# Score products of the cross-attention by seven of eight in passes two to four, with folded weights made beside V

## The chip, the cores and the metric

The kernel runs on one core of a Trainium2 chip. A core has a matmul engine (TensorE, "PE" in the profile, with its weight loads as "PEld"), VectorE ("DVE"), ScalarE ("ACT"), GpSimd ("POOL") and SyncE ("SP"). Each engine takes its own instructions in order; they meet through semaphores. Most transfers are issued by SP, one after the other. The metric is the device time of one execution in microseconds. Three runs before the change took 2639.5, 2645.52 and 2638.56 us, median 2639.5.

## The reference

One layer of a hybrid encoder over 2048 tokens of 1024 channels:

```
y = rmsnorm(h) @ w_in                       # 1024 -> 2560: q, k, v (8 heads of 64), u (conv, 2 x 512)
att = dilated_sliding_attention(q, k, v)    # three patterns, softmax over each band
conv = conformer_conv(...)                  # gate, 31-tap depthwise conv, layernorm, silu
h = h + concat(att, conv) @ w_out
xq = rmsnorm(h) @ w_xq                      # 4 heads of 256
sc = (xq . xk) / sqrt(256); pr = softmax(sc); xo = pr @ xv    # 256 memory rows
h = h + xo @ w_xo
h = h + square(relu(rmsnorm(h) @ w_up)) @ w_down              # 1024 -> 4096 -> 1024
return rmsnorm(h)
```

All is float32 at the interface. The memory rows do not depend on the tokens, so the kernel folds `w_xq` with the keys into one matrix A (1024 x 4 heads x 256) and the values with `w_xo` into one matrix B. The score products that the change is about are h times A.

## The kernel before, in words

A float32 product is made as three float16 products: high by high, high by low, low by high (`mm3`, lines 374 to 376). Each operand is split beforehand into a float16 part (ACT) and the rest (DVE).

The program has a first phase over all tokens and then four passes of 512 tokens.

- **First phase.** The memory is folded into A (kept in DRAM as `ascr`, two pairs of heads) and B (`bscr`). The linears for k, q, the conv input (`glu`) and v (`lin_v`) run as a pipeline of units that PE takes in order. Beside it DVE runs the first conv tile (`cacc`), and `scan` loads `w_up`, `w_out` and `w_down` once to sum squares, from which `bounds` makes the power-of-two scales of all splits (`S_A` for A). V tiles `v0_0` to `v1_7` end this phase; each is read out by ACT and DVE into `vst` and stored to `vtok`.
- **Attention of the first pass** (`att(0)`, three patterns). It starts in the memory that the first phase's tiles leave; its masked score operation on DVE reads the tile `mask`, which SP loads. The remaining linears (`frest`: `u0_2`, `u0_3` and others, and `v1_8` to `v1_15`) are woven between its steps.
- **A pass** (`post(p)`). Stage o: `cat @ w_out` plus the residual, with `y`, the split input of the score products, as output. Stage xs: scores, 192 products of 512 columns a pass, A's tiles loaded from `ascr` and split anew in each pass (`ws_a`, by `wpost`). Softmax, transposes (`ptx`). Stage x: `probabilities @ B` plus the residual. Then the MLP, up and down. The attention and conv of the next pass are woven between these steps as side work; the fourth pass has none.
- **Seven of eight.** The MLP's up products of passes two to four already use a 2 x 2 block scheme with seven block products instead of eight (`quad`). Its weights' block sums are made once by `prep` on ACT and DVE and stored as `ust`; its input's block sums are made when the input is (`columns`, `put_columns`: `B11`, `B2`, `T1`, `T32`, `T4`).
- **Ring of weight tiles.** `wtile` gives out four or seven slots in turn (`ws`, and `raw` as the last three). In the first pass split weights of the MLP are also stored (`wst`) for later passes; `save(n)` issues the stores that are due, all but the last n.

The program's order is not the order on the engines: a scheduler places the instructions of each engine, within limits that `pinned`, `after` and `weave(main, (side, rate))` set.

Of the kernel before, what the change touches and what calls it, by code (L numbers as in the profile page):

```python
# [10 lines left out]
F32 = mybir.dt.float32  # L11
# [10 lines left out]
P = 128  # L22
# [26 lines left out]
def hybrid_layer(ctx, tc, A, out):  # L49
# [70 lines left out]
    ust = [[dr.tile([P, 2 * 1024], F16, name=f"ust{fg}_{i}") for i in range(7)] for fg in range(8)]  # L120
# [26 lines left out]
    gxm = cst.tile([P, 24], F32, name="gxm")  # L147
# [5 lines left out]
    cst.tile([P, 56], F32, name="cpad")  # L153
# [101 lines left out]
    def bounds():  # L255
# [9 lines left out]
        with ExitStack() as st:  # L265
# [15 lines left out]
            TS(c[18], c[18], 16.0, None, op0=ALU.mult)  # L281
# [11 lines left out]
        with ExitStack() as st:  # L293
# [14 lines left out]
            TS(gxm[:, 16:24], gxm[:, 8:16], -1.0, None, op0=ALU.mult)  # L308
        yield
# [153 lines left out]


# [544 lines left out]
    with ExitStack() as st:  # L1009
# [10 lines left out]
        weave(islice(steps, 5), (conv0, 1.05), (scn, 2))  # L1020
        frest = [u for c in range(4) for u in glu(c, (2, 3), True)]
        for u in frest[:2] * 2:
            next(u)
        weave(steps, (conv0, 1.05), (scn, 2))
        drain(conv0, scn)
# [347 lines left out]
    def flat(t):  # L1373
        return t.rearrange("p h a b -> p (h a b)")

# [133 lines left out]
    def resid_linear(load, rhs, korder, resid, hs, ssum, scale, gains, y, name, steps=False, wide=False, put=None):  # L1509
# [26 lines left out]
    def prep(fgs, q):  # L1536

        late = []

        def give(d, t):  # L1540
            late.append((d, t))

        def step():
            for d, t in late:
                dma(d, t, q)
            late.clear()

        def hi(o, i):
            ACT.activation(o, i, AF.Copy, scale=S_UP)

        def lo(o, i, h):
            DVE.scalar_tensor_tensor(o, i, S_UP, h, op0=ALU.mult, op1=ALU.subtract)

        for fg in fgs:
            for j in range(2):
                nm = f"{fg}{j}"
                raw = [ct0.tile([P, 8, P], F32, tag=f"ch{i}", name=f"pw{i}_{nm}") for i in range(2)]
                step()
                for i in range(2):
                    dma(raw[i], wcols(w_up, (4 * fg + 2 * i + j) * P), q)  # L1560
                a11, a12, a21, a22 = (r[:, 4 * i:4 * i + 4] for r in raw for i in range(2))
                yield
                yield
                step()
                t0 = ct0.tile([P, 2, 8, P], F16, tag="cl0", name=f"pt0_{nm}")
                hi(t0[:, 0], raw[0])
                s1 = sw.tile([P, 4, P], F32, tag="s1", name=f"ps1_{nm}")
                DVE.tensor_tensor(s1, a21, a22, op=ALU.add)
                DVE.tensor_tensor(a21, a11, a21, op=ALU.subtract)
                yield  # L1570
                step()
                lo(t0[:, 1], raw[0], t0[:, 0])
                give(ust[fg][j], flat(t0))
                DVE.tensor_tensor(a11, s1, a11, op=ALU.subtract)
                t2 = ct0.tile([P, 2, 8, P], F16, tag="cl1", name=f"pt2_{nm}")
                hi(t2[:, 0], raw[1])
                yield
                step()
                DVE.tensor_tensor(a12, a12, a11, op=ALU.subtract)
                lo(t2[:, 1], raw[1], t2[:, 0])  # L1580
                give(ust[fg][4 + j], flat(t2))
                yield
                step()
                t1 = ct0.tile([P, 2, 8, P], F16, tag="cl0", name=f"pt1_{nm}")
                hi(t1[:, 0, 0:4], a11)
                hi(t1[:, 0, 4:8], s1)
                t3 = sw.tile([P, 2, 4, P], F16, tag="s4", name=f"pt3_{nm}")
                hi(t3[:, 0], a12)
                yield
                step()  # L1590
# [588 lines left out]
```

## Time and profile before

| | |
|---|---|
| runs, us | 2639.5, 2645.52, 2638.56 |
| profiled execution | 2644.86 us, of which the span 2643.0 |
| granted clock, mean | 0.995 |
| busy PE, DVE, ACT, POOL | 98%, 74%, 47%, 12% of the span |
| chain that ended last | PE 77%, DVE 12%, DMA 6% |
| stage o of passes 1 to 4 begins at, us | 668.0, 1192.6, 1699.3, 2191.5 |
| stage xs | 713.6, 1234.9, 1746.7, 2236.8 |
| stage x | 767.9, 1290.9, 1796.1, 2281.2 |

The busy time of PE counts products that overlap: a product of 512 columns lasts 379 ns in the records, but the next begins earlier. The distance between two starts is the price of a product, and PE's idle time is seen best in the timeline. A row of a stage's table gives the length of the stretch, the busy time of each engine with its count of instructions, the granted clock, the DMA engines' mean busy share and the rate.

### The profile page before, as it was taken

How to read it: one execution, taken by the hardware profiler on the slowest of the kernel's cores; microseconds unless marked ns; L12 is line 12 of the kernel's file. 1: busy time of each engine (PE TensorE's matmuls, PEld its weight loads, DVE VectorE, ACT ScalarE, POOL GpSimd, SP SyncE). 2: the span in 40 equal slices, each digit the busy share in tenths (PEclk: the TensorE clock that was granted, in tenths of full speed). 3: DMA queues.
4: the chain of work that ended last, by engine and by line, in shares of the span. 5: the costliest groups of instructions: out<-in, count | busy, mean ns of one | idle time of the engine just before them, and what ended most of it. 6: DMA issues, size and time to landing. Idle time of an engine off the chain costs nothing.

```text
span 2643.0 us, 45573 instructions
## 1 busy us (share of the span) xinstructions
PE 2588.1 (98%) x17710; PEld 1650.8 (62%) x17710; DVE 1947.6 (74%) x3775; ACT 1239.1 (47%) x2194; POOL 307.3 (12%) x417
## 2 busy tenths in 40 slices
PE   8999999999999999999999999999999999999998
PEld 7844448777455555545576676555776664468886
DVE  5887756567667999775799986467899557675666
ACT  5737645376454345544553344255443234452323
POOL 1134101132100110110001111000110000000000
PEclk9999999999999999999999999999999999999999
DMA  8987977766634657785367677454686465345442
GB/s 263 300 266 221 284 233 258 194 177 189 186 98 139 193 175 244 219 271 162 108 213 218 200 240 238 165 162 132 216 264 192 145 203 167 100 133 170 156 138 78
DMA packets 401753, 509.51 MB, mean 193 GB/s; under 512 B 81181, under 2 KB 295121, under 8 KB 400768
## 3 DMA queue, kind: packets, MB, share of 16 engines
q1 hardware_dynamic: 380816, 446.35, 55.3%
q0 software_dynamic: 15536, 51.24, 6.0%
q10 hardware_dynamic: 5184, 9.01, 0.9%
q8 instruction: 139, 2.28, 0.4%
q14 instruction: 78, 0.64, 0.1%
HBM read 390.75 MB, written 115.75 MB: 192 GB/s over the span
## 4 chain that ended last, share of the span: by engine, by line
PE 77%; DVE 12%; DMA 6%; issue 2%; ACT 2%; SPq 0%; POOL 0%; DVEq 0%; POOLq 0%; ACTq 0%
PE dn L375 7%; PE dn L376 7%; PE dn L374 7%; PE up L376 6%; PE up L375 6%; PE up L374 6%; PE lin L376 3%; PE lin L374 3%; PE lin L375 3%; DVE cacc L391 3%; PE xs L375 2%; PE xs L376 2%; PE xs L374 2%; PE pt L1047 2%; PE o L374 2%
## 5 line engine op out<-in xcount | busy, mean ns | idle before, releaser
L391 DVE SCALAR_TENSOR_TENSOR cacc<-cu,cw,cacc 128x512 f32<-128x512 f32 x480 | 364.4, 765 | 5.5
L375 PE MATMUL dn<-hhl,ws_d 128*128 128x512 f16 x768 | 290.6, 379 | 1.4 <-DVE hhl L1878 0.8
L374 PE MATMUL dn<-hhh,ws_d 128*128 128x512 f16 x768 | 287.9, 379 | 3.7 <-ACT hhh L1655 2.3
L376 PE MATMUL dn<-hhh,ws_d 128*128 128x512 f16 x768 | 290.5, 379 | 0.0
L1040 DVE CUSTOM_DVE_ANT_0 sm<-s,mask,qks 128x256 f32<-128x256 f32 (+1 forms) x384 | 151.1, 433 | 31.6 <-PE s L1081 28.0
L1041 ACT ACTIVATE sm<-sm,o 128x256 f32<-128x256 f32 (+1 forms) x288 | 119.3, 455 | 110.9 <-DVE o L1040 110.3
L1051 DVE TENSOR_TENSOR pl<-pt,ph 128x512 f16<-128x512 f32 x160 | 109.7, 685 | 42.1 <-ACT ph L1050 41.7
L374 PEld LDWEIGHTS <-ws_t 128*128 128x128 f16 x1232 | 120.6, 98 | 18.2 <-DMA ws_t<-ust 1.8
L376 PEld LDWEIGHTS <-ws_d 128*128 128x128 f16 x768 | 75.1, 98 | 90.4 <-issue 2.0
L375 PEld LDWEIGHTS <-ws_t 128*128 128x128 f16 x1232 | 120.5, 98 | 17.5 <-issue 2.3
L1050 ACT CAST ph<-pt 128x512 f16<-128x512 f32 x160 | 91.4, 571 | 84.5 <-PE pt L1047 84.3
L376 PEld LDWEIGHTS <-ws_t 128*128 128x128 f16 x1232 | 120.5, 98 | 16.8 <-issue 1.1
L374 PEld LDWEIGHTS <-ws_d 128*128 128x128 f16 x768 | 75.1, 98 | 84.7 <-issue 2.5
L375 PEld LDWEIGHTS <-ws_d 128*128 128x128 f16 x768 | 75.4, 98 | 83.7 <-issue 1.6
L1904 DVE SCALAR_TENSOR_TENSOR h<-dn,bd,h 128x512 f32<-128x512 f32 x96 | 71.5, 746 | 74.0 <-PE dn L376 73.7
L1047 PE MATMUL pt<-ident,sm 128*128 128x128 f32 x640 | 98.2, 274 | 4.6 <-ACT sm L1041 2.9
L374 PE MATMUL up<-mh,ws_u 128*128 128x512 f16 x256 | 98.1, 383 | 2.1 <-DVE rl L1875 2.1
L1687 ACT ACTIVATE e<-e 128x512 f32<-128x512 f32 x88 | 55.2, 629 | 95.3 <-DVE e L1685 95.3
L376 PE MATMUL up<-mh,ws_u 128*128 128x512 f16 x256 | 98.1, 384 | 1.3 <-DVE ws_u L362 1.3
L375 PE MATMUL up<-ml,ws_u 128*128 128x512 f16 x256 | 98.1, 383 | 0.0
L374 PE MATMUL up<-T32h,ws_t 128*128 128x256 f16 x352 | 95.9, 273 | 2.1 <-DMA ws_t<-ust 2.1
L374 PE MATMUL o<-cath,ws_o 128*128 128x512 f16 x256 | 96.5, 379 | 0.9 <-ACT cath L1219 0.8
(560 smaller groups left out, 7751.3 us busy)
## 6 DMA issues: line engine op xcount, KB each, us to landing
ws_t<-ust SPq DMA_DIRECT2D x154, 512.0 KB
ws_d<-wst SPq DMA_DIRECT2D x80, 512.0 KB
ust<-pt POOLq DMA_DIRECT2D x36, 512.0 KB, 5.1
scan<-in_w_up_dram SPq DMA_DIRECT2D x32, 512.0 KB
scan<-in_w_down_dram SPq DMA_DIRECT2D x32, 512.0 KB
raw_o<-in_w_out_dram SPq DMA_DIRECT2D x32, 512.0 KB
raw_a<-ascr SPq DMA_DIRECT2D x32, 512.0 KB
raw_b<-bscr SPq DMA_DIRECT2D x32, 512.0 KB
```

The source lines that it names most:

```text
L374: PE.matmul(o, lh, rh, start=first, stop=False, skip_group_check=more)
L375: PE.matmul(o, lh, rl, start=False, stop=False, skip_group_check=more)
L376: last["pe"] = PE.matmul(o, ll, rh, start=False, stop=end, skip_group_check=more)
L391: DVE.scalar_tensor_tensor(acc, u[:, t:t + 512], cw[:, c, t:t + 1], acc, op0=ALU.mult, op1=ALU.add)
L1040: last["dve"] = DVE.tensor_tensor_reduce(dst, so, mask[:, 256 * m:256 * m + nk], SCORE, 3e38, ALU.add, ALU.min, mn)
L1041: last["act"] = ACT.activation(dst, dst, AF.Exp, bias=mn, scale=-1.0)
L1047: last["pe"] = PE.transpose(pt[:, j, :], sm[:, j, :], ident)
L1050: ACT.copy(ph, pt)
L1051: DVE.tensor_tensor(pl, pt, ph, op=ALU.subtract)
L1687: ACT.activation(e, e, AF.Square)
L1904: last["dve"] = DVE.scalar_tensor_tensor(hs[m], pt, K_DN, hs[m], op0=ALU.mult, op1=ALU.add)
```

## The change

1. In passes two to four the score products go by seven block products of eight (`side_quad`), with 256 columns each. The input is made as column blocks (`columns(p, "s")`, `put_columns` with the gain columns of the cross norm), the softmax and the transposes work on blocks (`soft_block`, `turn_block`). Pass one is as before.
2. The block sums of A are made once, by `prep((8, 9))` in the first phase, beside the V products; their tiles are those of the q weights (`q0` to `q3`) and temporaries. `side_scale` makes `S_A` ahead of `bounds`, and A's bound is four times as large to leave room for the sums. They are stored as `ust[8]` and `ust[9]`.
3. The first pass's last split MLP tile is stored at the end of that pass (`save(0)`) instead of at the second pass's first MLP tile.

```
-    ust = [[dr.tile([P, 2 * 1024], F16, name=f"ust{fg}_{i}") for i in range(7)] for fg in range(8)]
+    ust = [[dr.tile([P, 2 * 1024], F16, name=f"ust{fg}_{i}") for i in range(7)] for fg in range(10)]
...
-            TS(c[18], c[18], 16.0, None, op0=ALU.mult)
+            TS(c[3], c[3], 4.0, None, op0=ALU.mult)
+            for i in (17, 18):
+                TS(c[i], c[i], 16.0, None, op0=ALU.mult)
...
+    def side_scale():
+        c = bd[:, 59:60]
...
+            PE.matmul(pc[:, 0:n], onesq, acc2[:, AS[0]:AS[1]], start=True, stop=True)
+            DVE.tensor_reduce(c, pc[:, 0:n], axis=AX.X, op=ALU.add)
+            DVE.tensor_scalar(c, c, 4.0, None, op0=ALU.mult)
+        yield
+        pow2(S_A, I_A, None, 32768.0, "dve", of=c)
...
     (prep, moved up and given an allocator; its new lines)
+                    if fg < 8:
+                        dma(raw[i], wcols(w_up, (4 * fg + 2 * i + j) * P), q)
+                    else:
+                        v = ascr[fg - 8].rearrange("p (h j k) n -> p h j k n", h=2, j=2)
+                        dma(raw[i].rearrange("p (h k c) m -> p h k (c m)", h=2, k=2),
+                            v[:, :, j, :, 256 * i:256 * i + 256], q)
...
+        def side_tile(tag, shape, dtype, name):
+            at = {"ch0": "q0", "ch1": "q1", "cl0": "q2", "cl1": "q3"}.get(tag)
+            return wqk.tile(list(shape), dtype, tag=at, name=name) if at else t2(name, dtype, shape)
+
+        side = pinned(chain(side_scale(), prep((8, 9), None, side_tile)), "dve", "act")
...
-        weave(steps, (conv0, 1.05), (scn, 2))
-        drain(conv0, scn)
+        weave(steps, (conv0, 1.05), (scn, 2), (side, 3))
+        drain(conv0, scn, side)
...
-        y = ytiles("y")
+        y = put = None
+        if p:
+            one, two_, side = columns(p, "s")
+            put = put_columns(one, two_, hs, 0, 24)
+        else:
+            y = ytiles("y")
...
+        def side_quad(hp, pth, ptl):
...
+            def prod(pt, w, n, more=False):
+                for t in range(2):
+                    ts_ = slice(P * t, P * t + P)
+                    for k in range(4):
+                        wh, wl = (x.rearrange("p (k c) m -> p k (c m)", k=2)[:, k % 2] for x in w[k // 2])
+                        mm3(halved(pt)[:, t], side[n]("h", k)[:, ts_], side[n]("l", k)[:, ts_], wh, wl,
+                            not (more or k or t), k == 3, bool(more or t))
...
+            def done(e, pt, i, z):
+                last["dve"] = DVE.tensor_tensor(e, e, pt, op=ALU.add)
+                soft_block(e, z)
+                late.append((pth, ptl, i, z, e))
...
+            prod(X, w11, "B11")
+            e1 = kept(X, "e1")
+            prod(Y, w12, "B21")
...
+            if p:
+                for _ in side_quad(hp, pth, ptl):
+                    if mlp and hp:
+                        next(mlp)
+                    yield
+                continue
...
         r = rstd_from(fsum)
+        save(0)
```

Where the instructions stand. First DVE at the end of the V phase, before the change: `vst1_7` is the read-out of the last V tile of the phase, `u0_2` and `u0_3` are the gated linears' read-outs, and the ISA row is the attention's first masked score (numbers behind the names are buffer numbers).

```order
L817 SCALAR_TENSOR_TENSOR vst1_6_5257<-v1_6_5232,vst1_6_5257 128x4x64
L817 SCALAR_TENSOR_TENSOR vst1_7_5287<-v1_7_5262,vst1_7_5287 128x4x64
L746 SCALAR_TENSOR_TENSOR u0_2_5418<-sig0_2_5362,lin_5391 128x512
L746 SCALAR_TENSOR_TENSOR u0_3_5446<-sig0_3_5389,lin_5421 128x512
L817 SCALAR_TENSOR_TENSOR vst1_8_5476<-v1_8_5449,vst1_8_5476 128x4x64
L1040 ISA sm_5519,o3_00_5518<-s_5520,mask_5306,qks_269 128x128
```

The same place on DVE after the change: `ps1_91`, `pw0_91`, `pw1_91` and `pt.._91` are the sums, the loaded blocks and the split results of the fourth and last unit of block sums.

```order
L525 TENSOR_TENSOR pw1_91_5398<-pw0_91_5397,pw1_91_5398 128x512
L503 SCALAR_TENSOR_TENSOR pt2_91_5410<-pw1_91_5398,bd_277,pt2_91_5410 128x1024
L503 SCALAR_TENSOR_TENSOR pt0_91_5403<-pw0_91_5397,bd_277,pt0_91_5403 128x1024
L530 TENSOR_TENSOR pw0_91_5397<-ps1_91_5405,pw0_91_5397 128x512
L535 TENSOR_TENSOR pw0_91_5397<-pw0_91_5397 128x512
L503 SCALAR_TENSOR_TENSOR pt3_91_5419<-pw0_91_5397,bd_277,pt3_91_5419 128x512
L503 SCALAR_TENSOR_TENSOR pt1_91_5416<-pw0_91_5397,bd_277,pt1_91_5416 128x512
L503 SCALAR_TENSOR_TENSOR pt1_91_5416<-ps1_91_5405,bd_277,pt1_91_5416 128x512
L838 SCALAR_TENSOR_TENSOR u0_2_5552<-sig0_2_5496,lin_5525 128x512
L838 SCALAR_TENSOR_TENSOR u0_3_5580<-sig0_3_5523,lin_5555 128x512
L909 SCALAR_TENSOR_TENSOR vst1_8_5610<-v1_8_5583,vst1_8_5610 128x4x64
L1137 ISA sm_5653,o3_00_5652<-s_5654,mask_5440,qks_283 128x128
```

All four units now stand ahead of the first masked score, the last two of them between `vst1_7` and `u0_2`.

Next SP's queue around the end of the V phase. Before, the mask stood among the stores of V's tiles, ahead of those of `vst1`:

```order
L58 DMA vtok_69<-vst0_14_4934 128x2x260
L58 DMA vtok_69<-vst0_15_4964 128x2x260
L58 DMA mask_5306<-in_masks_dram 128x1664
L58 DMA vtok_69<-vst1_0_5021 128x2x260
L58 DMA vtok_69<-vst1_1_5051 128x2x260
L58 DMA vtok_69<-vst1_2_5104 128x2x260
```

After the change, first the place behind the last V tile's store: the second unit's last stores, the load for the third unit (`pw0_90`), then what the attention begins with (V weights `wvr1`, keys `k3`, queries `ql3`, V rows `v3`, gate weights `wr_a12`).

```order
L58 DMA ust8_3_241<-pt1_81_5227 128x2048
L58 DMA vtok_69<-vst1_7_5371 128x2x260
L58 DMA ust8_6_244<-pt3_81_5230 256x1x512
L58 DMA pw0_90_5312<-ascr_253 128x4x256
L58 DMA wvr1_5473<-vscr_252 128x4096
L58 DMA k3_0_5628<-kscr_67 128x2560
L58 DMA ql30_5461<-qscr_68 64x2048
L58 DMA v3_0_5634<-vtok_69 128x4160
L58 DMA k3_1_5646<-kscr_67 128x2560
L58 DMA ql31_5462<-qscr_68 64x2048
```

And then, right behind these, the rest of the block sums and the mask:

```order
L58 DMA wr_a12_5590<-gscr3_113 128x2048
L58 DMA ust9_0_245<-pt0_90_5376 128x2048
L58 DMA ust9_4_249<-pt2_90_5383 128x2048
L58 DMA pw1_91_5398<-ascr_253 128x4x256
L58 DMA ust9_6_251<-pt3_90_5392 256x1x512
L58 DMA pw0_91_5397<-ascr_253 128x4x256
L58 DMA ust9_2_247<-pt1_90_5389 128x2048
L58 DMA ust9_5_250<-pt2_91_5410 128x2048
L58 DMA ust9_1_246<-pt0_91_5403 128x2048
L58 DMA ust9_6_251<-pt3_91_5419 256x1x512
L58 DMA ust9_3_248<-pt1_91_5416 128x2048
L58 DMA mask_5440<-in_masks_dram 128x1664
```

The mask has moved from the middle of V's stores to behind the last store of block sums. On PE the rows from the last V product of the phase to the first scores are the same as before: 96 products of the gated linears, the product of `v1_8` and half of `v1_9`.

227 lines of the change are left out of this document (149 added, 78 removed).

## The prediction

> **What bounds the kernel now.** I read the page's busy line and its chain, then PE's own timeline for what one product costs, then the stretches around the two places where the change puts work.
>
> ```profile
> span 2643.0 us, 45573 instructions
> PE 2588.1 (98%) x17710; PEld 1650.8 (62%) x17710; DVE 1947.6 (74%) x3775; ACT 1239.1 (47%) x2194; POOL 307.3 (12%) x417
> PE 77%; DVE 12%; DMA 6%; issue 2%; ACT 2%; SPq 0%; POOL 0%; DVEq 0%; POOLq 0%; ACTq 0%
> ```
>
> PE is busy nearly all the time and owns 77% of the chain. So a product taken away is worth its time, and a wait put in front of PE costs its time: hardly anything later can make up for it. The 379 ns that the groups give for a product is no price, since products overlap. The price is the distance between starts, here for 512 columns (15 rows, first and last) and for 256 (14 rows, first and last), with the weight load that goes with each:
>
> ```profile
> 1261.78 0.38 PE L375 MATMUL xs<-ws_a,yh 128*128 128x512 f16 x1
> ...
> 1264.80 0.38 PE L376 MATMUL xs<-ws_a,yl 128*128 128x512 f16 x1
> 454.48 0.27 PE L375 MATMUL v<-wv,xh 128*128 128x256 f16 x1
> ...
> 455.90 0.27 PE L376 MATMUL v<-wv,xl 128*128 128x256 f16 x1
> L374 PEld LDWEIGHTS <-ws_t 128*128 128x128 f16 x1232 | 120.6, 98 | 18.2 <-DMA ws_t<-ust 1.8
> ```
>
> 3.02 us over 14 steps is 0.2157 us; 1.42 over 13 is 0.109. Half the columns cost half the time, and a weight load of 98 ns still fits under 109.
>
> **Part 1, the score products.** One of three equal rows:
>
> ```profile
> L375 PE MATMUL xs<-ws_a,yh 128*128 128x512 f16 x256 | 97.0, 379 | 0.3 <-DVE ws_a L362 0.2
> ```
>
> Three rows of 256 are 768 products for four passes, 192 a pass. Passes two to four had 576 x 0.2157 = 124.2 us. Now each pass has 2 side quads x 7 products x 2 token tiles x 4 blocks of the sum x 3 = 336 of 256 columns: 1008 x 0.109 = 109.9. PE gains 14.3 us. The transposes are as many as before. The Trainium skill, "TensorE: Matmul & The Clock Gate" (Back-to-back issue gap), speaks against this step: it gives a stream of load and product pairs 131 ns a product at 512 columns and 81 at 128, so that an estimate of about 98 at 256 would turn 75 us into 99, 24 us slower. The trace does not agree (215.7 ns at 512), so the measured spacing decides.
>
> **Part 2, the block sums beside V.** This is where I see the cost. Four units (two side quads, two column halves) of the routine that already folds the MLP's weights:
>
> ```profile
> L1552 DVE SCALAR_TENSOR_TENSOR pt<-pw,bd,pt 128x1024 f16<-128x1024 f32 x32 | 40.6, 1273 | 0.3 <-ACT pt L1549 0.3
> L1552 DVE SCALAR_TENSOR_TENSOR pt<-pw,bd,pt 128x512 f16<-128x512 f32 x32 | 23.8, 744 | 1.7 <-ACT pt L1549 1.7
> L1568 DVE TENSOR_TENSOR ps<-pw 128x512 f32<-128x512 f32 x16 | 10.9, 683 | 0.0
> L1579 DVE TENSOR_TENSOR pw<-pw 128x512 f32<-128x512 f32 x16 | 11.7, 731 | 0.0
> L1549 ACT ACTIVATE pt<-pw,bd 128x1024 f16<-128x1024 f32 x32 | 36.4, 1142 | 28.9 <-DMA pw<-in_w_up_dram 23.4 <-DVE pw L1569 5.2
> ust<-pt POOLq DMA_DIRECT2D x36, 512.0 KB, 5.1
> ```
>
> A unit on DVE is 2 x 1.27 + 3 x 0.744 + 4 x about 0.70 = 7.6 us; four are 30 us. Each moves two loads of 512 KB, three stores of 512 and one of 256: 11.5 MB for all four. What stands there before:
>
> ```profile
> 440.00:475.00 35.00, 35.00 (x314) 30.54 (x312) 26.91 (x90) 11.49 (x25) 10.15 (x25) 1.00 0.69 194
> 475.00:498.00 23.00, 23.00 (x132) 12.38 (x130) 1.80 (x3) 1.76 (x3) 0.00 (x0) 1.00 0.93 260
> 454.30 0.35 SPq L58 DMA_DIRECT2D mask<-in_masks_dram  x1
> 473.58 0.42 DVE L817 SCALAR_TENSOR_TENSOR vst<-v,vst 128x256 f16<-128x256 f32 x1 [1.48 <-ACT vst L816]
> 498.01 0.35 DVE L1040 CUSTOM_DVE_ANT_0 sm<-s,mask,qks 128x128 f32<-128x128 f32 x1 [0.71 <-PE s L1081]
> 501.25 0.69 DVE L418 TENSOR_TENSOR lsum<-lc 128x512 f32<-128x512 f32 x1
> ```
>
> The columns of a stretch are its length, then busy us of PE, PEld, DVE, ACT and POOL, granted clock, DMA share and GB/s. On busy time alone 21 us of DVE are free from 475 to 498. But the work is not free to lie there, as the order shows (quoted with the change): all of the fourth unit stands on DVE ahead of the evictions u0_2 and u0_3, of vst1_8 and of the attention's first masked scores; and on SP the mask, issued at 454.3 before, now stands behind the last store of block sums. PE's row order between the last V product and the first scores is the same, so PE has nothing to put into a wait. A gain is excluded here for that reason.
>
> The chain, by hand. (a) The first two units, 15.2 us of DVE, stand ahead of or around the last V eviction, where 35 - 26.9 = 8.1 us were free: it slips from 473.6 to about 478 (474 to 481). (b) Unit three's second load can only be issued then, because its tile is the one that unit two reads: 5 us to land (the median of 5.1 above) and about 8 of unit: 491. (c) Unit four's load waits for unit three's sums, about 490, lands at 495 on an empty queue, and 8 us of unit end it at 503; the mask needs about 5 more: 508 against 498, a wait of 10. (d) The queue is not empty. Between these loads SP issues, by the answer on the DMA issues, what the attention starts with:
>
> ```profile
> k<-kscr SPq DMA_DIRECT2D x2, 640.0 KB
> v<-vtok SPq DMA_DIRECT2D x1, 1040.0 KB
> wvr<-vscr SPq DMA_DIRECT2D x1, 1024.0 KB
> ql<-qscr SPq DMA_DIRECT2D x2, 256.0 KB
> wr_a<-gscr SPq DMA_DIRECT2D x1, 512.0 KB
> 480.00:485.00 5.00, 5.00 (x24) 2.25 (x23) 0.00 (x0) 0.69 (x1) 0.00 (x0) 1.00 1.02 372
> ```
>
> That is 4.5 MB, with 2.9 MB of block loads and stores 7.4 MB up to unit four's own load, from about 480. At between 260 GB/s (the stretch from 475) and 372 (its best 5 us), 20 to 28 us: the load lands at 500 to 508, the unit ends at 508 to 516, and the mask lands some 6 us later, behind the last stores, at 514 to 522: a wait of 16 to 24. (e) Of the convolution's norm the sum `lsum`, 3.2 us behind the first scores, needs tiles that are loaded behind the mask and behind some V rows: 0 to 4 more. I take 22, near the contended end, because the stretch from 475 already had its DMA at 0.93; bounds 10 and 28. The Trainium skill, "DMA: Bandwidth & Descriptors" (Anatomy of one DMA), prices a transfer at 2.0 us plus its bytes at 436 GB/s, an estimate of 3.2 us for 512 KB; with it steps (b) and (c) would be about 6 us shorter. The row says 5.1, and I keep that.
>
> A wait of this length also costs clock:
>
> ```profile
> 539.24 0.38 PE L376 MATMUL lin<-xh,wr_g 128*128 128x512 f16 x1
> 541.59 0.44 PE L1047 MATMUL pt<-ident,sm 128*128 128x128 f32 x2 [1.97 <-ACT sm L1041]
> 540.00:550.00 10.00, 7.92 (x77) 5.76 (x78) 3.81 (x20) 8.35 (x19) 7.71 (x8) 0.83 0.76 232
> ```
>
> After an idle stretch of 2 us the clock over 10 us is 0.83, 1.7 us lost. After 22 us I put 2 (bounds 1.7 and 3.4, twice that).
>
> **Part 3, passes two to four.** The input of the score products is now made as column blocks, as in
>
> ```profile
> L1634 DVE SCALAR_TENSOR_TENSOR B11l<-h,gxm,B11h 128x256 f16<-128x256 f32 x12 | 5.7, 476 | 0.0
> L1639 DVE SCALAR_TENSOR_TENSOR t<-h,gxm,t 128x256 f32<-128x256 f32 x12 | 5.8, 481 | 0.2
> L1643 DVE TENSOR_TENSOR B2l<-yv,B2h 128x512 f16<-128x512 f32 x12 | 8.2, 684 | 0.0
> L1644 DVE TENSOR_TENSOR yv<-yv,t 128x256 f32<-128x256 f32 x12 | 5.0, 417 | 0.0
> L1532 DVE SCALAR_TENSOR_TENSOR yl<-h,gxm,yh 128x512 f16<-128x512 f32 x32 | 23.2, 745 | 0.4 <-ACT yh L1531 0.4
> L362 DVE SCALAR_TENSOR_TENSOR ws_a<-raw_a,bd,ws_a 128x1024 f16<-128x1024 f32 x32 | 40.9, 1280 | 16.0 <-ACT ws_a L361 16.0
> 2220.00:2240.00 20.00, 20.00 (x94) 9.07 (x93) 18.29 (x23) 12.60 (x16) 0.00 (x0) 1.00 0.59 180
> 2280.00:2300.00 20.00, 18.33 (x92) 9.01 (x91) 10.13 (x26) 9.30 (x24) 0.00 (x0) 1.00 0.15 49
> ```
>
> Per pass on DVE: four tiles at 0.42 + 2 x 0.476 - 0.745 = 0.6, four at 2 x 0.48 + 2 x 0.684 + 2 x 0.417 - 0.745 = 2.4, eight block sums at 0.68 = 5.5, less eight splits of `ws_a` at 1.28 = 10.2: 7 us more in about 100 us, hidden under the products where DVE is half free (10.1 of 20 us in the last row). The loads go from 8 x 512 KB to 14 a pass, at a DMA share of 0.15 there. Without that cover 7 us a pass would show. In passes two and three the next pass's attention also fills PE; in the fourth nothing does, and there two seams are new: the second product needs all eight tiles of the input, and the output weights come right behind the quads. The nearest row is the old seam, 20 - 18.33 = 1.7 us of idle PE; I take 2 for both (bounds 0 and 8).
>
> **Part 4, the early store.**
>
> ```profile
> 1315.18 10.43 DMA wst<-ws_d
> 1320.00:1345.00 25.00, 25.00 (x163) 14.30 (x162) 21.05 (x45) 14.42 (x26) 0.81 (x1) 1.00 0.64 203
> ```
>
> The old late store held back a weight split for 10 us, but PE was busy for all of the stretch from 1320, with attention. I put nothing (up to 1 us of gain).
>
> **The sum.** -14.3 + 22 + 2 + 2 = +11.7. The profiled execution took 2644.86 us (span 2643.0 and 1.9 around it): 2656.6. That run lies 5.4 us over the median of 2639.5, so beside the median the forecast is 2651.2. About 0.3%, 8 us, is what a measurement of this kernel can tell from no change.
>
> **The rivals.** (1) The fourth unit gets through in time, and the attention starts no more than 3 us late. The mechanism is the free DVE stretch from 475 and full-rate transfers; for it speak those 21 us and the unchanged PE order, against it two loads and two units in series. The point that decides is whether the mask lands before 501. Then -14.3 + 1.5 = about -13: 2626.5, faster. (2) The wait is there but short, 7 to 15 us, because transfers do not queue and DVE does not fall behind (step c alone): with 11, -14.3 + 11 + 2 + 2 = +0.7: 2640. (3) The forecast's wait, and 10 us on top, in the seams of passes two to four, where DVE in order runs the new column blocks of the next input ahead of what PE waits for: 2661. For it: DVE had 18.3 of 20 us to do in the stretch from 2220, where the fourth pass's input is made; against it, that PE idled only 1.7 us at the old seam, and that the splits leave.
>
> **How the numbers follow.** Forecast 0.55, of which 0.06 lies below 8 us; rival 1 0.17; rival 2 0.18, with all but 0.01 within 8 us; rival 3 0.10. Faster by over 0.3%: 0.17. Within: 0.17 + 0.06 = 0.23. Slower: 0.49 + 0.10 + 0.01 = 0.60. The forecast's own range, waits of 14 to 28 us, is 2643 to 2657. With rival 2's (from 2636) and a part of each end, 2630 to 2664 holds about 0.8; a little more than 0.1 lies below and some 0.07 above.
>
> **What would show it.** Right: in the changed profile the score products of passes two to four start 0.109 us apart; in the stretch from 475 to 530 PE has some 22 us of idle time ended by DVE or the mask, with a half clock behind it; the first masked scores come at about 520; the last V eviction at about 478; later stages about 5 us a pass shorter. Wrong: first masked scores by 502 (rival 1) or by 510 (rival 2), or idle PE of over 5 us between the products of a side quad (rival 3).

## The result and the profile after

The changed kernel took 2678.4 us, the median of four runs from 2672.4 to 2681.7, against 2639.6 for the kernel before: 1.014 times as long (95% interval 1.0116 to 1.0163). Slower was forecast, but by 12 us and not by 39, and the time lies above the 2630 to 2664 of the forecast. The profiled execution took 2672.44 us, its span 2670.7: 27.7 us more than the span before. That profile is of the fastest run of the new kernel, the one before of a run 5 us over its median, so the traces explain 28 of the 39 us. What the other runs of the new kernel lose beyond that stands in no trace.

The busy line of the page, and the table of stretches around the end of the V phase (length, then busy us of PE, PEld, DVE, ACT and POOL, granted clock, DMA share, GB/s):

```profile
span 2670.7 us, 46728 instructions
PE 2575.2 (96%) x18144; PEld 1689.9 (63%) x18144; DVE 1990.3 (75%) x3904; ACT 1266.7 (47%) x2262; POOL 307.5 (12%) x418
440.00:475.00 35.00, 34.57 (x299) 29.06 (x298) 27.63 (x76) 15.41 (x30) 4.67 (x16) 1.00 0.78 221
475.00:482.00 7.00, 6.99 (x33) 3.06 (x32) 5.40 (x18) 2.21 (x4) 0.99 (x1) 1.00 0.87 279
482.00:519.00 37.00, 0.00 (x0) 0.00 (x0) 18.64 (x37) 7.71 (x10) 4.72 (x9) 0.54 0.84 267
519.00:535.00 16.00, 15.93 (x83) 8.51 (x83) 3.44 (x6) 2.20 (x5) 0.00 (x0) 0.88 0.72 203
```

PE does nothing at all for 37 us, and then still has 16 us of work ahead of the first scores. The waits of that place, in order of time, with the engine's idle time and what ended it in brackets:

```profile
481.29 0.41 DVE L909 SCALAR_TENSOR_TENSOR vst<-v,vst 128x256 f16<-128x256 f32 x1
491.85 1.51 SPq L58 DMA_DIRECT2D ust<-pt  x2
505.26 0.72 ACT L500 ACTIVATE pt<-pw,bd 128x512 f16<-128x512 f32 x1 [10.15 <-DMA ust<-pt]
507.79 0.69 DVE L524 TENSOR_TENSOR ps<-pw 128x512 f32<-128x512 f32 x1 [0.37 <-DMA pw<-ascr]
511.80 0.69 DVE L525 TENSOR_TENSOR pw<-pw,pw 128x512 f32<-128x512 f32 x1 [3.32 <-DMA pw<-ascr]
517.72 0.72 ACT L500 ACTIVATE pt<-pw,bd 128x512 f16<-128x512 f32 x1 [2.96 <-DVE pw L535]
518.35 1.25 ACT L835 ACTIVATE sig<-lin,wsc 128x512 f32<-128x512 f32 x2
519.07 0.59 PE L391 MATMUL lin<-xh,wr_a 128*128 128x512 f16 x1 [37.08 <-ACT sig L835]
522.05 0.42 SPq L58 DMA_DIRECT2D mask<-in_masks_dram  x1
535.61 0.35 DVE L1137 CUSTOM_DVE_ANT_0 sm<-s,mask,qks 128x128 f32<-128x128 f32 x1 [0.71 <-PE s L1178]
```

The first row is the last read-out of V. In the second the store of unit three's first tile is issued; in the third ACT gets that tile free only at 505.3, 13.4 us later, where the row that the forecast used has 5.1 for such a store. Unit four's first load is in at 507.8 (DVE has then waited 0.37 us for it), its second at 511.8. ACT then stands in order: the sigmoid `sig` of a gated linear comes behind unit four's roundings, at 518.35. Until it has read its bank of results, PE cannot go on with the next linear: the 37.08 us. So PE stopped not at the mask, as forecast, but 16 us of its own work ahead of the mask, and ran those 16 us after the stop. The first masked score, at 498.0 before, is at 535.6 on DVE, released by PE and not by the mask, which was issued at 522.05.

Where the 27.7 us come from, by starts of products in the two timelines (products at their regular distance count as work, the rest as idle):

| PE | before, us | after, us | difference | forecast |
|---|---|---|---|---|
| work | 2549.4 | 2535.8 | -13.6 | -14.3 |
| idle up to the first scores | 36.5 | 74.0 | +37.5 | +22 |
| idle and half clock, first pass's attention | | | +2.0 | +2 |
| idle, end of the scores of pass four | 0.5 | 8.7 | +8.2 | +2, for all seams |
| idle ahead of stage o of passes two and three | | | -1.2, -3.6 | 0 |

These rows add up to 29.3 us; the remaining stages together take 1.6 us less than before, which leaves the 27.7. Which gap between two products is idle is a choice, so the first row is good to about 1 us.

The products themselves cost what was forecast, here of a side quad (27 rows, first and last):

```profile
2284.12 0.27 PE L392 MATMUL xs<-ws_s,B11h3s 128*128 128x256 f16 x1
...
2286.96 0.27 PE L393 MATMUL xs<-ws_s,T4l3s 128*128 128x256 f16 x1
```

2.84 us over 26 steps is 0.109.

### The profile page after: what moved, and what is told of

Same layout as the page of the kernel before. It is cut to its first block, busy times and chain, and to the rows that moved or that the text cites. A ratio compares the mean times of both kernels' runs of the same rounds, so it can differ in the third digit from the quotient of the medians.

```text
span 2670.7 us, 46728 instructions
## 1 busy us (share of the span) xinstructions
PE 2575.2 (96%) x18144; PEld 1689.9 (63%) x18144; DVE 1990.3 (75%) x3904; ACT 1266.7 (47%) x2262; POOL 307.5 (12%) x418
## 5 line engine op out<-in xcount | busy, mean ns | idle before, releaser
L500 ACT ACTIVATE pt<-pw,bd 128x1024 f16<-128x1024 f32 (+1 forms) x80 | 74.0, 928 | 93.0 <-DMA ust<-pt 28.9
```

The costliest lines, as they stand in the source:

```text
L500: ACT.activation(o, i, AF.Copy, scale=S_UP if fg < 8 else S_A)
```

## The experiments

Each edit is given against the changed kernel where nothing else is said. "Stage o" is the first product of the first pass's output linear: 668.0 us before, 707.6 after, 39.6 late. "Scores" is the first masked score, 0.2 us ahead of its row on DVE: 497.8 and 535.4. (Stage o, too, is given some 0.3 us ahead of its first product's row.) Unlike the ratios, these come from one trace each. In the five traces below that have nothing but the scale beside V, the row of stage o's first product stands at 664.9 to 665.7, for 668.3 before the change: some 3 us of difference against the kernel before come without any block sums. In the kernels with the block sums' stores, sums or both left out (`no_stores`, `no_sums`, `no_sums_pool`, `sums_only`), the new products read other block sums of the same size, as in `quads_only`.

### Which part costs

The block sums and their stores alone, with the old score products (`v_only`):

```
-            if p:                                  # columns, side_quad
+            if False:
...
-        save(0)
```

> The kernel before with the block sums beside V alone; the score products of all passes as they were, no early store. My theory after the trace: the whole loss is made between 481 and 535 us of the changed kernel, so the first masked scores come 36 to 39 us later than before (about 535) and the time is 36 to 42 us over before, 2676 to 2682. Rival: part of the loss is made in passes two to four (the changed kernel's runs lie up to 10 us over its profile); then this one costs 25 to 30 us only.

The new products without the block sums (`quads_only`): they read other, equally large block sums.

```
-        side = pinned(chain(side_scale(), prep((8, 9), None, side_tile)), "dve", "act")
+        side = pinned(side_scale(), "dve", "act")
...
-                dma(flat(t), ust[8 + hp][i])
+                dma(flat(t), ust[hp][i])
```

> The change without the block sums beside V: the side quads read the folded tiles of the first two MLP groups in place of their own (that part of the computation is replaced, the work is the same), the early store stays. My theory: passes two and three gain 4 to 5 us each at the quads and 1 to 3 behind them, the fourth loses 4 at its first products and wins 2 back: 8 to 13 us less than before, 2627 to 2632. Rival: the quads are no gain at all because the seams eat them: within 4 us of before.

The early store alone, in the kernel before (`save0`):

```
         r = rstd_from(fsum)
+        save(0)
```

> The kernel before with the early store alone. I had put 0 to 1 us of gain. In the traces with it the stretch from the second pass's output of the cross attention to the third pass's start took 404 to 407 us, without it 408.1 and 408.5. Theory: 1 to 4 us less, 2637 to 2641 beside 2641; rival: those came from the side quads, and this one is at 0, with 408 us in that stretch.

Measured: `v_only` 1.016 (1.0146 to 1.0174), scores at 536.4, stage o at 708.1: the whole loss is there with no new product in the kernel. `quads_only` 0.9975 (0.9964 to 0.9986), 8 us faster, scores at 495.2. `save0` 0.9991 (0.9978 to 1.0003): not to be told from nothing, as Part 4 had it. So the products are worth 7 to 8 us as built (3.7 to 9.5 by the interval), less than their 13.6 of work; a row of `quads_only` says where a part goes, in the last pass:

```profile
2240.66 0.39 PE L391 MATMUL xs<-ws_s,T4h3s 128*128 128x256 f16 x1 [3.26 <-ACT T4h3s L1678]
```

### What the wait consists of

Three suspects: the tile that waits for its store's landing, the bytes, and the roundings ahead of the sigmoid. A separate buffer for that tile (`own_t1`):

```
-                t1 = alloc("cl0", (P, 2, 8, P), F16, f"pt1_{nm}")
+                t1 = alloc("cl2", (P, 2, 8, P), F16, f"pt1_{nm}")     # "cl2" is "q4"
```

> The changed kernel with a buffer of its own for the third pair of tiles of a block-sum unit, so that ScalarE needn't wait until the first pair's store has landed (10.2 us in unit three of the changed kernel's trace). Theory A (the chain inside the units sets the length): the first masked scores come about 10 us earlier, 524 to 527, and the time falls by 8 to 11, to 2664 to 2671 beside 2639.5. Theory B (bytes: block sums and the attention's first loads go through one queue of full DMA engines, 11.5 MB more at about 280 GB/s): nothing to win, first scores at 531 to 536, time within 4 us of the changed kernel.

No stores of block sums, 7.3 MB less (`no_stores`):

```
-            late.append((d, t))
+            if fg < 8:
+                late.append((d, t))
```

> The changed kernel without the stores of the block sums beside V (7.3 of their 11.5 MB); the side quads read the MLP's folded tiles instead (that part of the computation is replaced). Theory B (bytes): 7.3 MB at 280 GB/s are 26 us, so the first masked scores come at 507 to 514 and the time is 22 to 28 us under the changed kernel's: 2650 to 2657. Theory A (units in series, each with two loads and 8 us of VectorE and ScalarE work): only the stores' landing goes, first scores at 520 to 526, time 10 to 15 under: 2663 to 2668.

The roundings on GpSimd instead of ACT, so that the sigmoid stands behind nothing (`pool_hi`):

```
     def hi(o, i):
+        if fg == 9:
+            POOL.tensor_scalar(o, i, S_A, None, op0=ALU.mult)
+            return
```

> The changed kernel with the last two units' roundings to 16 bits on GpSimd in place of ScalarE (10 instructions moved; TensorE's and VectorE's orders are the same). It takes away what stands ahead of the two sigmoids for which TensorE stopped at 481.6. Theory A (16 us of linears and V rows stand behind that stop): TensorE runs on to about 492, the stop gets 10 us shorter, and the first pass's output linear (707.6 in the changed kernel) starts 7 to 10 us earlier. Theory B (bytes): the stop moves, but the convolution's tiles still land when they landed, and the output linear starts within 3 us of 707.6 (later, if GpSimd's roundings hold up the units).

`own_t1`: 1.014 (1.0126 to 1.0153), scores at 535.2. ScalarE waited as long for a store one step later, and the sigmoid was as late as before; the DMA engines had been full meanwhile:

```profile
510.25 0.72 ACT L500 ACTIVATE pt<-ps,bd 128x512 f16<-128x512 f32 x1 [10.76 <-DMA ust<-pt]
517.87 1.25 ACT L835 ACTIVATE sig<-lin,wsc 128x512 f32<-128x512 f32 x2
498.00:510.00 12.00, 0.00 (x0) 0.00 (x0) 2.87 (x5) 1.44 (x2) 0.00 (x0) 0.50 1.02 357
```

So this one buffer is not the cause. `no_stores`: 1.0094 (1.0074 to 1.0114), scores at 525.6, stage o at 694.0. 13.6 of the 39.6 us go with the stores. 26 remain, and the sigmoid is still late, now behind unit three's and four's loads:

```profile
488.98 2.19 ACT L501 ACTIVATE pt<-pw,bd 128x1024 f16<-128x1024 f32 x2 [13.24 <-DMA pw<-ascr]
507.85 1.25 ACT L836 ACTIVATE sig<-lin,wsc 128x512 f32<-128x512 f32 x2
```

`pool_hi`: 1.0172 (1.0155 to 1.0189), slower still, with stage o at 716.4. PE ran on to 491.9, but stopped then for as long, since the gated linears' second read-out, on DVE, stands behind the units too:

```profile
528.22 0.37 PE L391 MATMUL v<-wvr,xh 128*128 128x256 f16 x1 [36.34 <-DVE u L841]
547.12 0.69 DVE L435 TENSOR_TENSOR lsum<-lc 128x512 f32<-128x512 f32 x1 [9.79 <-DMA lc<-cscr]
```

### Transfers and arithmetic apart

The same loads and stores, with no sums made (`no_sums`):

```
-        side = pinned(chain(side_scale(), prep((8, 9), None, side_tile)), "dve", "act")
+        side = pinned(chain(side_scale(), transfers()), "dve", "act")
...
     (in transfers, in place of each sum, one element that ties a store to its load)
+                        DVE.tensor_scalar(ts[i][:, 0, 0, 0:1], raw[r][:, 0, 0:1], 0.0, None, op0=ALU.mult)
```

> The changed kernel with every load and store of the block sums beside V, in their order and each waiting for the same tiles, but without their arithmetic (30 us of VectorE, 22 of ScalarE): single columns of zeros are written in its place, and the side quads read the MLP's folded tiles (that part of the computation is replaced). Theory B (transfers alone, bytes through full DMA engines): first masked scores stay at 530 to 536, output linear of the first pass at 702 to 708. Theory C (a chain of units in series whose links are arithmetic, store landing and load; taking the stores away won 10 us of 38, so each kind of link holds a part): 8 to 14 us earlier, first scores at 521 to 527, output linear at 693 to 700. Theory A (arithmetic of the last two units sets it): 16 us or more, first scores by 519.

The same with GpSimd's queue for these transfers (`no_sums_pool`), and the changed kernel itself with them there (`pool_q`):

```
-        prep((8, 9), None, side_tile)
+        prep((8, 9), POOL, side_tile)
```

> All four units' loads and stores beside V without their arithmetic (single columns of zeros in its place, the side quads on the MLP's tiles), issued from GpSimd's queue in place of SyncE's. On SyncE's queue the mask then held up the first scores until 520 and the convolution's tiles VectorE until 530: output linear at 696.7. Theory D (order in SyncE's queue): output linear at 670 to 682. Theory B (bytes): 691 to 700.

> The changed kernel with the block sums' loads and stores beside V issued from GpSimd's queue; TensorE's order is the same, VectorE's and ScalarE's nearly. Theory D with the chain of theory C: mask and convolution tiles come in time, but the sigmoids and evictions still stand behind the fourth unit, which lands no earlier; first masked scores at 528 to 535, output linear at 697 to 705. Theory B (bytes alone): within 3 us of the changed kernel (output linear at 705 to 711). If the order on SyncE were all, the output linear would come by 685.

The sums, with tiles that are filled on the chip in place of loads, and no stores (`sums_only`):

```
     (with the store's condition of no_stores)
-                        dma(raw[i].rearrange("p (h k c) m -> p h k (c m)", h=2, k=2),
...
+                        POOL.memset(raw[i], 0.0)
```

> The changed kernel with the whole arithmetic of the four units beside V but none of their loads and stores: the raw tiles are set to zero by GpSimd, nothing is stored, and the side quads read the MLP's folded tiles (that part of the computation is replaced). It is the counterpart of the run that kept the transfers alone, where the first pass's output linear came 26 us later than before (693.9 against 668.0). If transfers and arithmetic each fill time of their own, the arithmetic alone costs the rest of the 39.6: output linear at 678 to 684, 10 to 16 late. If the arithmetic fits into VectorE's free 21 us from 475 (the forecast's first rival): 667 to 672. If it is in the chain with its full length: 690 or more.

| | median, us | ratio (95%) | scores, us | stage o, us | late at stage o |
|---|---|---|---|---|---|
| transfers alone, SP's queue | 2671.8 | 1.0112 (1.0092 to 1.0132) | 520.4 | 696.7 | 28.7 |
| transfers alone, GpSimd's queue | 2664.7 | 1.0094 (1.0074 to 1.0113) | 522.7 | 693.9 | 25.9 |
| arithmetic alone | 2655.0 | 1.0056 (1.0038 to 1.0074) | 513.4 | 683.3 | 15.3 |
| both, GpSimd's queue | 2675.8 | 1.0131 (1.0111 to 1.0150) | 534.8 | 705.8 | 37.8 |
| both, SP's queue | 2678.4 | 1.0140 (1.0116 to 1.0163) | 535.4 | 707.6 | 39.6 |

Compared on the same queue, 28.7 + 15.3 is 44.0 and both together make 39.6 on SP's; 25.9 + 15.3 is 41.2 and both make 37.8 on GpSimd's. So the two mostly add: of the 15.3 us some 11 to 12 come on top of the transfers, where work that ran fully beside them would add nothing. (Counted from the 665 of the kernels without block sums beside V, the arithmetic alone is 18 us late, and the same 11 to 12 come on top.) The 15.3 are rather too many than too few, since in that kernel ScalarE also waits 2.9 and 2.3 us for GpSimd to fill the tiles of the last two units. The queue that issues is worth 2 to 3 us in these traces, and the intervals of the ratios overlap. With transfers alone PE runs the linears while the bytes move, and the mask does end the wait, at 520.6, close to the forecast's own 520:

```profile
520.60 0.35 DVE L1168 CUSTOM_DVE_ANT_0 sm<-s,mask,qks 128x128 f32<-128x128 f32 x1 [5.44 <-DMA mask<-in_masks_dram]
530.19 0.69 DVE L435 TENSOR_TENSOR lsum<-lc 128x512 f32<-128x512 f32 x1 [7.11 <-DMA lc<-cscr]
```

With arithmetic alone, the stop at the sigmoid is there without a load or store of the units:

```profile
497.34 0.58 PE L391 MATMUL lin<-xh,wr_a 128*128 128x512 f16 x1 [13.96 <-ACT sig L834]
```

With both, and the transfers on GpSimd's queue (`pool_q`), the mask no longer stands behind them. It is issued 34 us earlier than in the changed kernel, and the stop is there all the same:

```profile
488.16 0.44 SPq L58 DMA_DIRECT2D mask<-in_masks_dram  x1
517.93 0.59 PE L391 MATMUL lin<-xh,wr_a 128*128 128x512 f16 x1 [34.66 <-ACT sig L835]
535.08 0.35 DVE L1137 CUSTOM_DVE_ANT_0 sm<-s,mask,qks 128x128 f32<-128x128 f32 x1 [0.72 <-PE s L1178]
```

An early mask is worth half a microsecond at the scores (535.08 for 535.61): in the changed kernel it is not the mask that PE and DVE wait for. On that queue, without arithmetic, the DMA share stays at 1 for 35 us (stretches of the second kernel of the table):

```profile
485.00:498.00 13.00, 9.48 (x44) 4.21 (x43) 0.97 (x4) 0.00 (x0) 5.56 (x12) 0.97 0.99 356
498.00:510.00 12.00, 8.79 (x56) 6.71 (x56) 1.84 (x6) 0.77 (x2) 2.33 (x4) 0.74 1.02 348
510.00:520.00 10.00, 0.00 (x0) 0.00 (x0) 0.31 (x2) 0.00 (x0) 1.45 (x4) 0.55 1.04 305
```

This is the part that another queue did not remove: the block sums' bytes and the attention's first tiles want the DMA engines at the same time. The Trainium skill, "Trainium Kernel Development and Optimization" (Key Constraints), says that DMAs from the queues of SP, ACT and GpSimd run on the same 16 engines and interleave, and that several issuers save only issue time. The runs agree for all four units: 2.8 us between the two queues with transfers alone, 1.8 us in the whole kernel. With half of the sums the queue was worth 6 us, as the next section shows: there the order mattered too.

### Another place for the block sums

Half of them beside V, half at the end of pass one (`half`), the same with GpSimd's queue (`half_pool`), and all of them in the first pass's later part (`moved`):

```
-        ... prep((8, 9), None, side_tile)
+        ... prep((8,), None, side_tile)     # half;   POOL for None: half_pool;   none: moved
...
+        preps = {0: (9, 0, 1), ...}         # half, half_pool;   moved: {0: (8, 9, 0, 1), ...}
...
     (the rate of that side work in the first pass, 0.9 before: 1.2 in half and half_pool, 1.5 in moved)
```

> The changed kernel with only the first side quad's two units beside V; the second quad's two units stand in the first pass, ahead of the MLP's two groups. My theory: the first two units were done by 482 in the changed kernel and nothing waited for them, so the first masked scores come within 3 us of before (498 to 501) and the sum is the quads' gain less 0 to 8 us for 15 us of DVE more in the first pass: 2628 to 2637. Rival (any block load or store beside V holds up the attention's loads, by bytes): half of the wait stays, first scores at 512 to 518, time 2645 to 2652.

> The kernel with half of the block sums beside V (the first quad's two units), those units' loads and stores issued from GpSimd's queue in place of SyncE's. With half the sums on SyncE's queue the first masked scores came at 499.3, but VectorE then waited 14.3 us for the convolution's tiles, which were issued at 503.7 in place of 484.7. Theory D (the order in SyncE's queue): the tiles are issued by about 488 again and that wait goes: first pass's output linear at 669 to 675 in place of 684.8. Theory B (bytes: the DMA engines are full from 485 to 510, whoever issues): the wait stays, output linear at 680 to 686.

> The changed kernel with all four units of block sums in the first pass, ahead of the MLP's two groups, at a higher rate; nothing beside V but the scale. My theory: the wait at 481 goes whole; 30 us of DVE more in the first pass, where DVE is 96% busy from 870 to 1060 and 70% after: 0 to 10 us of new waits there; 2628 to 2639. Rival: the first pass is bound by DVE there, so that all 30 us show: 2655 to 2660.

All of them beside the first pass's scores and transposes (`early`):

```
+        sums = pinned(prep((8, 9), None, pass_tile), "dve", "act")
+        weave(islice(main, 21), *sides, (sums, 1.0))
```

> The changed kernel with all four units of block sums in the first pass beside the score products and the output of the cross attention (from about 713 to 900 us), where the DMA share is 0.38 to 0.48 and VectorE is 70% busy; nothing beside V but the scale. Theory B (bytes where DMA is full): there the 11.5 MB are free; the gain of the quads alone remains, 8 to 13 us under before: 2628 to 2634, output linear of the second pass at 1184 to 1192. Rival (VectorE, 96% busy from 870 to 1060, and the work it pushes on): 10 to 20 us appear in the first pass again: 2640 to 2655.

In pass two, with the old products there and the new ones in passes three and four only (`late`), with the softmax steps kept ahead of the next input's:

```
-            if p:
+            if p > 1:
...
+        preps = {1: (3, 5, 6, 7, 8, 9), ...}
```

> Side quads in passes three and four only; their block sums stand in the second pass behind the MLP's four groups (from about 1580 us, where VectorE is 56% busy and the DMA share falls from 0.80 to 0.51), nothing beside V but the scale, and the last pass's hold as in the other kernel. My theory: 2 x 4.8 us of products are won, 0 to 5 of them lost again: 2630 to 2637. Rival (block sums cost 20 us wherever they stand, since TensorE has no slack in any stage): 2645 to 2655.

`quads_only` with the MLP's next step held behind the scores on DVE (`quads_pin`):

```
                     if mlp and hp:
-                        next(mlp)
+                        with ExitStack() as st:
+                            after(st, "dve")
+                            next(mlp)
```

> The kernel without block sums beside V (side quads on the MLP's tiles, as before: the work is the same), and with the last pass's first MLP steps held behind the side quads' sums on VectorE, so that four subtractions and four splits no longer stand ahead of the score products' input. My theory: the 8 to 9 us of idle TensorE between the last pass's score products go to 1 to 2, and the time is 6 to 8 us under that of the same kernel without the hold (2634.4): 2626 to 2629. Rival: the steps only come to stand ahead of something else (the second product's softmax, the first MLP products): within 3 us of 2634.

`half`: 1.0116 (1.0099 to 1.0133), where I had expected it faster than before. The first masked score was on time, at 499.5, but DVE then stood for the conv's tiles (`lc`), whose loads were issued at 503.7, for 484.7 before:

```profile
499.51 0.35 DVE L1137 CUSTOM_DVE_ANT_0 sm<-s,mask,qks 128x128 f32<-128x128 f32 x1 [0.71 <-PE s L1178]
503.74 2.00 SPq L58 DMA_DIRECT2D lc<-cscr  x4
517.14 0.69 DVE L435 TENSOR_TENSOR lsum<-lc 128x512 f32<-128x512 f32 x1 [14.32 <-DMA lc<-cscr]
```

`half_pool`: 1.0079 (1.0056 to 1.0102). That wait shrank to 9.44 us and stage o came 6 us earlier, at 678.6: order is a part of this one, and the rest fits the bytes, which no run took apart here. The V phase is not all of the loss of `half` either: in its trace stage o of the first pass is 17 us late and that of the second pass 26.

`moved`: 1.0091 (1.0078 to 1.0105). The V phase is as fast as before (stage o at 665.1), and stage o of pass two 24 us late. There too the place was not free; the row of its last 87 us in that pass shows the DMA share at 0.92 and PE idle for about 15:

```profile
1130.00:1217.00 87.00, 71.38 (x328) 33.82 (x327) 66.51 (x107) 44.31 (x59) 9.83 (x18) 0.91 0.92 292
```

`early`: 1.0066 (1.0052 to 1.0080). Here transfers had room, and still the profiled run took 2655.4 us for 2644.9. The stretch that takes up the sums (first row before, second row `early`):

```profile
768.00:818.00 50.00, 49.58 (x309) 26.71 (x306) 36.58 (x71) 29.17 (x54) 0.20 (x1) 1.00 0.38 106
768.00:820.00 52.00, 47.93 (x294) 25.39 (x294) 42.81 (x84) 35.22 (x64) 0.20 (x1) 1.00 0.53 154
```

The DMA share is only 0.53; DVE goes from 73% to 82% busy, and PE has 4 us free of 52 where it had 0.4 of 50. Behind it, ahead of stage o of pass two, PE idles 20.5 us for 10.3. So it is not bytes here; that it is DVE's order is the nearest reading, and no run takes it alone.

`late`: 2648.4, 1.0037 (1.0023 to 1.0050), the best place found and still slower; 12.89 us of idle PE stand at the end of pass two, in one gap that a DVE step ends. `quads_pin`: 2634.4, 0.9975 (0.9963 to 0.9988), no better than without the hold. The idle time in the last pass's scores fell from 9.2 to 2.0 us and 6.5 came back where the MLP's output follows: DVE has that work to do at one place or the other. No version beats the kernel before with its block sums made.

## Why the prediction was right in sign and wrong in size

- **What bounds it, part 1.** Right: -13.6 measured for -14.3, by the distance of starts. The two distances of 0.2157 and 0.109 us came back in the changed kernel. At the 81 and 131 ns that the prediction names beside it, no such gain would have come.
- **Part 2, step a.** The last read-out of V stands at 481.3 for 478, at the upper bound of 481.
- **Step b failed.** Unit three ended at 507.4, not 491: its middle tile waited for a store that landed in 13.4 us and not in 5.1. The 5.1 is the median of 36 stores on GpSimd's queue elsewhere in the program; it was used for SP's queue in a stretch with a DMA share of 0.84. Taking that one wait away (`own_t1`) won nothing, so this wait was not the cost by itself.
- **Step d was some 4 to 6 us short.** Unit four's loads landed at 507.8 and 511.8 (500 to 508 said), its last operation on DVE ended at 521.7 (508 to 516 said), and the mask was issued at 522.05. At the 5 us that it took in the run of transfers alone (issued at 515.6, read at 520.6) the mask landed, by this estimate, near 527 (514 to 522 said): a wait of about 29 by the mask alone, for the 22 taken and the upper bound of 28.
- **The step that failed in the sum** is the end of the chain, "the mask lands at 514 to 522: a wait of 16 to 24". I let units, transfers and linears run beside each other and took the mask as the last of them. It is not the last: with the mask issued at 488 (`pool_q`) the scores come half a microsecond earlier. The runs show 28.7 us for the transfers alone, more than what I took as the whole (22), and 15.3 for the arithmetic alone, and that most of the second comes on top. The trace shows how: the sigmoid stands behind unit four on ACT, so PE stopped at 482.0 with 16 us of linears and V products still to do, and did them only after 519. The idle time was 37.5 for 22, and measured from a mask at 527 the work behind the stop is some 8 of these 15 us. The sentence "PE's row order is the same, so PE has nothing to put into a wait" was true and half used: the same order also means that PE stops at the first read-out that is late, not at the last. The other 7 are the late mask of step d, that is, the loads that come later behind each unit's arithmetic and stores; this fits the rows, but no run took it alone.
- **Step e and the clock.** `lsum` waited 1.4 us after a late score in the changed kernel, inside 0 to 4. The half clock behind the stop cost 16 x (1 - 0.88) = 1.9 us by the row from 519, for 2.
- **Part 3.** Passes two and three showed no seam in the changed kernel, as said (in `quads_only` a wait of 2.06 us for an input block, `B2h11s`, stands in pass two). The last pass showed 8.2 us for 2, at the upper bound of 8; this is the third rival's kind of cost at one place, DVE in order. The fourth pass's place before and after, and the rows of one of its waits:

```profile
2242.00:2260.00 18.00, 17.94 (x88) 8.62 (x87) 14.74 (x27) 6.61 (x13) 1.01 (x1) 1.00 0.41 139
2267.00:2285.00 18.00, 12.14 (x93) 9.65 (x90) 16.20 (x28) 8.00 (x14) 1.12 (x1) 0.81 0.28 97
2275.95 1.27 DVE L379 SCALAR_TENSOR_TENSOR ws_d<-b,bd,ws_d 128x1024 f16<-128x1024 f32 x1
2277.15 1.21 DVE L2126 TENSOR_TENSOR b<-b,mask 128x1024 f32<-128x1024 f32 x1
2278.28 1.27 DVE L379 SCALAR_TENSOR_TENSOR ws_d<-mask,bd,ws_d 128x1024 f16<-128x1024 f32 x1
2279.92 0.41 ACT L1678 CAST T4h3s<-yv 128x256 f16<-128x256 f32 x1 [3.24 <-DVE yv L1676]
2280.38 0.40 PE L391 MATMUL xs<-ws_s,T4h3s 128*128 128x256 f16 x1 [3.25 <-ACT T4h3s L1678]
```

  The first row is the same place before, 18 us of work for PE; in the second it works 12.14, at a clock of 0.81, with DVE 90% busy. DVE runs block differences and splits of the MLP's weights (`b`, `ws_d`) for 3.5 us ahead of the last step of the input block `yv`; ACT waits for that step, and PE for ACT. So the rival had the engine right, but what stands ahead are weights of the MLP and not columns of the next input.
- **Part 4.** Nothing that a run can tell from zero (0.9991, 0.9978 to 1.0003), as said.
- **The rivals.** The first (free DVE from 475) and the second (no queueing) fell: the scores came at 535, not by 502 or 510.
- **Open.** What costs the other three runs of the changed kernel 5 to 9 us over the profiled one.

## What to carry to other kernels

When work is put beside a stage, list for every engine in order what stands behind it, and find the first read-out that the busiest engine waits for: the wait begins there, and the work that the busiest engine still has queued comes on top of it. Do not count on transfers and engine work of the added units to overlap when each load waits for a tile that the sums free: here 28.7 and 15.3 us made 39.6, nearer to the sum than to the larger one. Before planning 11.5 MB and 30 us of VectorE to win 14 us of products, look for a place where the DMA share and VectorE are both free; here five places were tried and there was none.

## What the runs showed of the hardware

- A store of 512 KB, which landed in 5.1 us on GpSimd's queue (median of 36 over the program), needed about 13.4 on SP's in the stretch with the DMA share at 0.84. In the stretches shown here with a share of 0.99 to 1.04 the rate was 305 to 357 GB/s.
- VectorE was slower while GpSimd worked. In `pool_hi` the fused operation of 128x1024 took 1708 ns on average where the changed kernel has 1282, while GpSimd's rounding took 2845 ns for what ACT does in 1.1 us:

```profile
L506 DVE SCALAR_TENSOR_TENSOR pt<-pw,bd,pt 128x1024 f16<-128x1024 f32 x4 | 6.8, 1708 | 4.9 <-POOL pt L501 4.9
L501 POOL TENSOR_SCALAR pt<-pw,bd 128x1024 f16<-128x1024 f32 x4 | 11.4, 2845 | 6.0 <-DVE pw L528 5.6 <-DMA pw<-ascr 0.4
L503 DVE SCALAR_TENSOR_TENSOR pt<-pw,bd,pt 128x1024 f16<-128x1024 f32 x4 | 5.0, 1282 | 1.7 <-ACT pt L500 1.7
```

  The first two rows are of `pool_hi`, the third of the changed kernel. The four operations of `pool_hi` lasted 2.14, 1.28, 2.13 and 1.28 us: the two long ones began just behind the start of a rounding on GpSimd, the two others when none was running, as here the first two:

```profile
489.66 5.69 POOL L501 TENSOR_SCALAR pt<-pw,bd 128x1024 f16<-128x1024 f32 x2 [0.39 <-DMA pw<-ascr]
492.56 2.14 DVE L506 SCALAR_TENSOR_TENSOR pt<-pw,bd,pt 128x1024 f16<-128x1024 f32 x1 [1.16 <-POOL pt L501]
496.07 1.28 DVE L506 SCALAR_TENSOR_TENSOR pt<-pw,bd,pt 128x1024 f16<-128x1024 f32 x1
496.25 2.53 POOL L501 TENSOR_SCALAR pt<-pw,bd 128x512 f16<-128x512 f32 x1 [0.90 <-DVE pw L538]
506.47 1.56 POOL L501 TENSOR_SCALAR pt<-ps,bd 128x512 f16<-128x512 f32 x1
```

  GpSimd was slower where it began inside an operation of VectorE: 2.53 us at 496.25, where the same form took 1.56 at 506.47. The Trainium skill, "SBUF — State Buffer" (SBUF: two separate sides), says that a VectorE operation with two SBUF inputs and a GpSimd operation that reads SBUF take turns at a shared pair of ports, held for a whole instruction. The rows agree that the two slow each other. They do not show a whole instruction waited out on VectorE's side: its operation from 492.56 ended at 494.70, before the roundings did at 495.35. No run here separates the ports from other causes.
